# Token-major openings in 512-column halves for four feed-forward blocks and a state-space block on one Trainium2 core

## The chip, the cores and the metric

The kernel runs on one core of a Trainium2 chip. The time is the device time of one execution in microseconds (us), lower is better. Three executions of the kernel before took 1203.37, 1204.36 and 1206.2 us, a median of 1204.36 us. The profile is one further execution.

## What is computed

A decoder trunk of four layers on x of 256 tokens by 1024 features, all in float32. Each layer is a token mixer and then a feed-forward block, both behind an RMSNorm and added to x. The mixers are stick-breaking attention (layers 0 and 3), a chunked spatial gate (layer 1) and a diagonal state-space layer, S5 (layer 2). What the change touches is this part:

```python
def causal_depthwise_conv(h, w, b):
    L = h.shape[1]
    hp = jnp.pad(h, ((0, 0), (CONV_K - 1, 0), (0, 0)))
    y = hp[:, 0:L] * w[0]
    for kk in range(1, CONV_K):
        y = y + hp[:, kk:kk + L] * w[kk]
    return y + b

def conv_gated_ffn(xn, w_up, conv_w, conv_b, w_down):
    h = causal_depthwise_conv(xn @ w_up, conv_w, conv_b)
    a, g = jnp.split(h, 2, axis=-1)
    return (jax.nn.silu(g) * a) @ w_down

def s5_layer(xn, w_in, ...):
    u = (xn @ w_in).astype(jnp.float32)
    ...
    _, _, xr, xi = lax.associative_scan(_complex_affine_combine, (a_re, a_im, bu_re, bu_im), axis=1)
    ...
    hg = jax.nn.gelu(y).astype(xn.dtype) @ w_glu
    a, g = jnp.split(hg, 2, axis=-1)
    return a * jax.nn.sigmoid(g)
```

`w_up` is 1024 x 5632, `w_down` 2816 x 1024, the S5 `w_in` 1024 x 1024.

## The kernel before

**Precision.** Every large product is made of three float32r matmuls: weights and activations are each split into a high part (`wh`, `xth`, `gh`) and the rest (`wl`, `xtl`, `gl`), and high x high, high x low and low x high are added up in PSUM. ScalarE (ACT) makes `wh` from the loaded weights `raw` (L71), VectorE (DVE) makes `wl` (L72), for half of a weight chunk (128 x 1024) at a time.

**Weights.** The class `Weights` streams chunks of 128 x 2048 floats (1 MB), in the order in which the phases use them, through three `raw` buffers and six `wh`/`wl` pairs. `take()` names the next chunk; `prep_to`, `half_to` and `step` put the splitting of later chunks into the program, and with it the DMA of the chunk after. Nothing is scheduled by a planner: each engine runs its instructions in the order in which the Python code issues them, and semaphores connect the engines.

**Phases.** `K.run` goes through eight phases (attention, feed-forward, gate, feed-forward, S5, feed-forward, attention, feed-forward). Each has an opening (`head`, once per block of 128 tokens, b = 0 and b = 1), a `body`, and a `tail` that interleaves its last products with the norm of the next phase. In the opening of block 0, `mid()` puts the transposes of block 1's normed input into the middle. A matmul's output goes to one of eight PSUM banks of 128 x 512 floats.

**Feed-forward.** The 5632 columns of `w_up` are 22 chunks "u" of 256 columns: chunk m holds 128 columns of the half `a` (s = 0) and 128 of the half `g` (s = 1). From chunk 4 on a chunk is projected feature-major (`proj_feat`: the weights are the stationary operand, 256 tokens the moving one; 24 matmuls of 256 columns for each s) into one of the banks 4 to 7, in rotation. The order is u4 u5 d0 u6 u7 d1 ..., where "d" is a chunk of `w_down` (`down`, 24 matmuls of 512 columns), accumulated in banks 0 to 3. The first three chunks are projected token-major instead (`proj_tok`: 128 tokens stationary, 256 weight columns moving, 24 matmuls of 256 columns for each block), so that block 0 can begin before block 1 is normed. Their results are copied from PSUM to two tiles `tk` (L362, L363) and turned to feature-major by PE transposes (L368, four per chunk) into banks 4, 5 and 6, in the middle of the fourth chunk's `proj_feat`.

`evac` takes chunks out of PSUM: per chunk two ACT instructions with the bias (L406), four on DVE for the convolution (L410), then silu, product and the split into `gh`/`gl` (L416, L417, L198, L199). Weight halves (L71 on ACT, L72 on DVE) are issued between those steps. The bank of a chunk is free after its last L410. `evac` of a chunk is issued one step after its projection.

**S5.** The opening is that of the feed-forward for three chunks of `w_in`. In `body` the fourth chunk goes to bank 7 feature-major, with the transposes of the first three into banks 4, 5 and 6 in its middle. 48 copies (`ucopy`, L1222 on DVE and L1224 on ACT) then regroup the state-space rows from PSUM into two tiles `U` of 128 x 1024: 16 on ACT and 16 on DVE for the first, 16 on ACT for the second. `gmm(i)` (L1140) multiplies quarter i of them with tables, into banks 0 and 1 for even i and 2 and 3 for odd i. `scan(i)` is a chain of DVE instructions (L1156 to L1167), with one tile `mg` that ACT writes (L1147); `kmm`, `kd`, `kevac` build a kernel matrix, `ymm` and `yevac` the output, and `glu` the gated projection.

Of the kernel before, what the change touches and what calls it, by code (L numbers as in the profile page):

```python
# [326 lines left out]
class FFN(Phase):  # L327
# [10 lines left out]
    def open(self):  # L338
# [8 lines left out]
        self.hb = [(7, 4), (2, 3)]  # L347

    def head(self, b, mid):
        k = self.k  # L350
# [7 lines left out]
        if b == 0:  # L358
            self.tk = []
        tk = k.xn_p.tile([128, D], F32, tag="xn", name="tk")  # L360
        self.tk.append(tk)
        self.nc.scalar.activation(tk[:, 0:512], k.bank(self.hb[b][0]), AF.Copy)  # L362
        self.nc.scalar.activation(tk[:, 512:768], k.bank(self.hb[b][1])[:, 0:256], AF.Copy)  # L363

    def transposes(self, m, p):
        for b in range(2):
            for s in range(2):
                self.nc.tensor.transpose(p[:, 256 * s + 128 * b:256 * s + 128 * b + 128],  # L368
                                         self.tk[b][:, 256 * m + 128 * s:256 * m + 128 * s + 128],
                                         self.k.ident[:, :])  # L370
# [1009 lines left out]
```

## Time and profile before

| | |
|---|---|
| median of three executions | 1204.36 us |
| the profiled execution | 1203.6 us |
| its span, first to last instruction | 1201.8 us |
| PE busy | 1179.5 us |
| DVE busy | 892.8 us |
| ACT busy | 709.3 us |

The span leaves out 1.8 us of the profiled execution. PE is TensorE's matmuls, PEld its weight loads, which run beside the matmuls. [...] In rows of the timeline the columns are start, duration (from the first start to the last end where a row stands for several), engine, line, operation, output <- inputs, shapes and count; a bracket at the end tells how long the engine had been idle and what ended it. The four feed-forward phases begin at about 133, 395, 696 and 1005 us, S5 at 585 us.

### The profile page before, as it was taken

To read this page: it belongs to the slowest core of one execution; us is meant where nothing else is said; L and a number is where in the kernel's file an instruction comes from. 1 tells how busy PE (TensorE), PEld (TensorE's weight loads), DVE (VectorE), ACT (ScalarE), POOL (GpSimd) and SP (SyncE) were. 2 spreads that over 40 slices of the span, in tenths; PEclk is the share of its full clock that TensorE was granted. 3 is DMA by queue.
4 is the path that set the end of the run, shared out by engine and by line. 5 is a ranking of instruction groups with operands and counts; after the bars stand their busy time and mean duration, and the time that the engine had idled before them with its cause. 6 is when DMAs were issued, how large, how long until landed. Compare 5 with 4: busy or idle time off the path is not lost. (4 is left out here: it accounts for less than half of the span.)

```text
span 1201.8 us, 21989 instructions
## 1 busy us (share of the span) xinstructions
PE 1179.5 (98%) x9072; PEld 1078.9 (90%) x9072; DVE 892.8 (74%) x1272; ACT 709.3 (59%) x1080; POOL 152.8 (13%) x293
## 2 busy tenths in 40 slices
PE   8999999999999999999987999999999999999997
PEld 5898999999898999999976899999988989999996
DVE  5665689799767599899669759777765656886673
ACT  5665576557564564667466657556545655665551
POOL 2886000000186001000100000000000000000000
PEclk9999999999999999999999999999999999999999
DMA  8633367786655466777862646644535333565530
GB/s 297 225 106 123 132 217 282 238 308 252 245 209 182 152 222 219 227 267 259 318 250 73 261 160 218 225 179 172 199 142 204 106 124 122 203 240 180 206 124 35
DMA packets 49557, 237.46 MB, mean 198 GB/s; under 512 B 14896, under 2 KB 15792, under 8 KB 24240
## 3 DMA queue, kind: packets, MB, share of 16 engines
q1 hardware_dynamic: 46208, 223.73, 51.9%
q0 software_dynamic: 3104, 12.06, 2.5%
q8 instruction: 71, 1.16, 0.4%
q14 instruction: 30, 0.25, 0.1%
q10 hardware_dynamic: 144, 0.26, 0.1%
HBM read 222.79 MB, written 13.24 MB: 196 GB/s over the span
## 5 line engine op out<-in xcount | busy, mean ns | idle before, releaser
L72 DVE TENSOR_TENSOR wl<-raw,wh 128x1024 fp32r<-128x1024 f32 x344 | 413.6, 1227 | 56.7 <-ACT wh L71 56.6
L124 PE MATMUL pst<-xth,wh 128*128 128x256 f32 x1552 | 441.0, 284 | 0.0
L125 PE MATMUL pst<-xtl,wh 128*128 128x256 f32 x1552 | 439.1, 283 | 0.0
L126 PE MATMUL pst<-xth,wl 128*128 128x256 f32 x1552 | 439.1, 283 | 0.0
L71 ACT ACTIVATE wh<-raw 128x1024 fp32r<-128x1024 f32 x344 | 350.2, 1048 | 9.5 <-DMA raw<-in_up_dram 3.9
L124 PEld LDWEIGHTS pst<-xth,wh 128*128 128x128 f32 x1552 | 297.7, 192 | 2.3
L125 PEld LDWEIGHTS pst<-xtl,wh 128*128 128x128 f32 x1552 | 297.8, 192 | 1.2
L126 PEld LDWEIGHTS pst<-xth,wl 128*128 128x128 f32 x1552 | 297.7, 192 | 0.0
L410 DVE SCALAR_TENSOR_TENSOR y<-pst,cw,y 128x255 f32<-128x255 f32 x352 | 160.7, 479 | 72.8 <-ACT y L406 66.6
L132 PE MATMUL pst<-wh,gh 128*128 128x512 f32 x512 | 201.3, 393 | 0.0
L133 PE MATMUL pst<-wl,gh 128*128 128x512 f32 x512 | 199.8, 390 | 0.0
L134 PE MATMUL pst<-wh,gl 128*128 128x512 f32 x512 | 199.3, 389 | 0.0
L406 ACT ACTIVATE y<-pst,cw 128x256 f32<-128x256 f32 x176 | 88.0, 556 | 69.5 <-PE pst L126 64.9
L134 PEld LDWEIGHTS pst<-wh,gl 128*128 128x128 f32 x512 | 96.1, 188 | 20.4
L132 PEld LDWEIGHTS pst<-wh,gh 128*128 128x128 f32 x512 | 96.3, 188 | 19.5 <-issue 0.3
L133 PEld LDWEIGHTS pst<-wl,gh 128*128 128x128 f32 x512 | 96.3, 188 | 18.4 <-DVE wl L72 0.2
L132 PE MATMUL pst<-wh,xth 128*128 128x256 f32 (+1 forms) x336 | 105.9, 315 | 0.0
L134 PE MATMUL pst<-wh,xtl 128*128 128x256 f32 (+1 forms) x336 | 105.4, 314 | 0.0
L133 PE MATMUL pst<-wl,xth 128*128 128x256 f32 (+1 forms) x336 | 105.3, 313 | 0.0
L163 POOL TENSOR_TENSOR r<-m,mhalf 128x1 f32<-128x1 f32 x20 | 11.0, 552 | 730.5 <-DVE m L161 730.5
L198 ACT ACTIVATE gh<-y 128x256 fp32r<-128x256 f32 x88 | 36.1, 418 | 75.5 <-DVE y L417 75.5
L416 ACT ACTIVATE y<-y 128x256 f32<-128x256 f32 x88 | 36.4, 419 | 73.6 <-DVE y L410 73.4
(167 smaller groups left out, 1202.7 us busy)
## 6 DMA issues: line engine op xcount, KB each, us to landing
raw<-in_up_dram SPq DMA_DIRECT2D x88, 1024.0 KB, 4.9
raw<-in_down_dram SPq DMA_DIRECT2D x44, 1024.0 KB, 4.9
raw<-in_wqk_dram SPq DMA_DIRECT2D x16, 1024.0 KB, 4.9
raw<-in_wo_dram SPq DMA_DIRECT2D x8, 1024.0 KB, 4.7
raw<-in_glu_dram SPq DMA_DIRECT2D x8, 1024.0 KB, 6.1
raw<-in_wv_dram SPq DMA_DIRECT2D x7, 1024.0 KB, 4.9
gb<-in_g_dram SPq DMA_DIRECT2D x9, 512.0 KB, 5.6
d_gt<-gf POOLq DMA_DIRECT2D x4, 1024.0 KB, 7.8
```

What stands on the lines that cost most here:

```text
L71: nc.scalar.activation(h[:, s], r[:, s], AF.Copy)
L72: nc.vector.tensor_tensor(out=l[:, s], in0=r[:, s], in1=h[:, s], op=ALU.subtract)
L124: nc.tensor.matmul(out, h[:, cols], xh, start=first, stop=False, skip_group_check=True)
L125: nc.tensor.matmul(out, h[:, cols], xl, start=False, stop=False, skip_group_check=True)
L126: nc.tensor.matmul(out, l[:, cols], xh, start=False, stop=last, skip_group_check=True)
L132: nc.tensor.matmul(out, ah, h[:, cols], start=first, stop=False, skip_group_check=True)
L133: nc.tensor.matmul(out, ah, l[:, cols], start=False, stop=False, skip_group_check=True)
L134: nc.tensor.matmul(out, al, h[:, cols], start=False, stop=last, skip_group_check=True)
L198: self.nc.scalar.activation(g[0][:, j], src, AF.Copy)
L406: nc.scalar.activation(y[:, cs], p[:, cs], AF.Identity, scale=cw[:, s, m, 2:3], bias=cw[:, s, m, 3:4])
L410: nc.vector.scalar_tensor_tensor(y[:, o + tap:o + 256], p[:, o:o + 256 - tap], cw[:, s, m, 2 - tap:3 - tap], y[:, o + tap:o + 256], ALU.mu ...
L416: nc.scalar.activation(y[:, 256:512], y[:, 256:512], AF.Silu)
```

## The change

The first four chunks of each `w_up`, and all of the S5 `w_in`, are packed in another way: instead of 256 columns by all eight k-tiles, a 1 MB chunk now holds 512 columns by four k-tiles. All four are projected token-major with `proj_half` (which the attention and the gate used before): 12 matmuls of 512 moving columns for each chunk and block, two chunks for 512 features. The names of the lines below are those of the changed kernel; L419, L423, L429 and L430 in it are L406, L410, L416 and L417 of the kernel before, L360 is the copy L362, L372 is the transpose L368, and L366 is a new copy in the new `rest`.

```diff
     def head(self, b, mid):
...
         for c in range(3):
-            p = k.bank(self.hb[b][c // 2])
-            k.proj_tok(self.hn[c], b, p[:, 256 * (c % 2):256 * (c % 2) + 256])
+            k.proj_half(self.hn[c], c % 2, b, k.bank(self.vb[b][c // 2]))
             if c == 1:
                 mid()
...
-        self.nc.scalar.activation(tk[:, 0:512], k.bank(self.hb[b][0]), AF.Copy)
-        self.nc.scalar.activation(tk[:, 512:768], k.bank(self.hb[b][1])[:, 0:256], AF.Copy)
+                self.tk.append(k.xn_p.tile([128, D], F32, tag="xn", name="tk"))
+                self.nc.scalar.activation(self.tk[b][:, 0:512], k.bank(self.vb[b][0]), AF.Copy)
+
+    def rest(self, n, b, out):
+
+        p = self.k.bank(self.vb[b][1])
+        self.k.proj_half(n, 1, b, p)
+        self.nc.scalar.activation(out, p, AF.Copy)
...
     def body(self):
...
+        def part(m, bank):
+            self.transposes([t[:, 256 * m:256 * m + 256] for t in self.tk], k.bank(bank))
+            pend.append((m, k.bank(bank)))
+
         for kind, a in self.order()[3:-3]:
             n = w.take()
-            if kind == "u":
-                p = k.bank(4 + a % 4)
+            if kind == "u" and a == 3:
+                self.rest(n, 0, self.tk[0][:, 512:1024])
+                part(0, 5)
+                part(1, 6)
+                self.rest(n, 1, self.tk[1][:, 512:1024])
+                e = []
+            elif kind == "u":
+                p = k.bank(7 if a == 4 else 4 + (a - 3) % 4)
                 k.proj_feat(n, p, 0)
-                if a == 3:
-                    for m in range(3):
-                        self.transposes(m, k.bank(4 + m))
-                        pend.append((m, k.bank(4 + m)))
+                if a == 4:
+                    part(2, 4)
+                    part(3, 5)
                 k.proj_feat(n, p, 1)
                 e = [(a, p)]
...
 class S5(Phase):
-    tb = (0, 1)
+    tb = (2, 3)
...
     def body(self):
-        ut = k.pst[:, 4:8, :].rearrange("p b (a t) -> p (b a) t", a=2)
+        mg = self.tmp.tile([128, 8, 64], F32, name="mg")
+        xs = [[self.tmp.tile([128, 8, 64], F32, name=f"x{i}{r}") for r in range(2)] for i in range(2)]
+        ut = [k.pst[:, b:b + 2, :].rearrange("p b (a t) -> p (b a) t", a=2) for b in (0, 5)]
+        tb = [t[:, :, :].rearrange("p a c -> p (a c)") for t in xs[1]]
...
         n = w.take()
-        k.proj_feat(n, k.bank(7), 0)
-        for m in range(3):
-            FFN.transposes(self, m, k.bank(4 + m))
-        k.proj_feat(n, k.bank(7), 1)
+        FFN.rest(self, n, 0, tb[0])
+        for m in range(2):
+            FFN.transposes(self, [t[:, 256 * m:256 * m + 256] for t in self.tk], k.bank(m))
+        new_u()
+        ucopy(0, slice(0, 2), on_act)
+        ucopy(0, slice(2, 4), nc.vector.tensor_copy)
+        FFN.rest(self, n, 1, tb[1])
...
-        gb = lambda i, r: k.bank(2 * (i % 2) + r)
+        gb = lambda i, r: k.bank(2 - 2 * (i % 2) + r)
...
-        ucopy(0, slice(0, 2), on_act)
-        ucopy(0, slice(2, 4), nc.vector.tensor_copy)
         gmm(0)
+        for m in range(2):
+            FFN.transposes(self, [t[:, 256 * m:256 * m + 256] for t in tb], k.bank(5 + m))
...
         ucopy(1, slice(0, 4), on_act)
         kmm(0)
         gmm(1)
         scan(0, lambda: (kd(0), kevac(0)))
...
-        acc = [(k.bank(0), k.bank(1)), (k.bank(4), k.bank(7))]
+        acc = [(k.bank(2), k.bank(3)), (k.bank(4), k.bank(7))]
...
-        self.acc = [(k.bank(2), k.bank(3)), (k.bank(5), k.bank(6))]
+        self.acc = [(k.bank(0), k.bank(1)), (k.bank(5), k.bank(6))]
```

The first place is ACT's queue where the first feed-forward body begins, before the change. Square brackets name the semaphores that the instruction waits for; `tk_1682` is the token-major tile of block 1, `y_1753`, `y_1760` and `y_1767` are chunks 0, 1 and 2.

```order
L362 ACTIVATE tk_1682<-pst_81 128x512 [waits DVE_49,PE_49]
L363 ACTIVATE tk_1682<-pst_81 128x256 [waits PE_49]
L71 ACTIVATE wh21_1685<-raw21_1600 128x1024 [waits DMAHW1_49]
L71 ACTIVATE wh21_1685<-raw21_1600 128x1024
L406 ACTIVATE y_1753<-pst_81,cw_1505 128x256 [waits PE_49,DMAHW0_49,Activation_49,Pool_49]
L406 ACTIVATE y_1753<-pst_81,cw_1505 128x256
L406 ACTIVATE y_1760<-pst_81,cw_1505 128x256 [waits PE_49]
```

The same place with the change (`tk_1543` and `tk_1597` are blocks 0 and 1, `y_1653` and `y_1660` chunks 0 and 1):

```order
L360 ACTIVATE tk_1597<-pst_81 128x512 [waits DVE_49,PE_49]
L71 ACTIVATE wh21_1611<-raw21_1563 128x1024 [waits DMAHW1_49]
L71 ACTIVATE wh21_1611<-raw21_1563 128x1024
L366 ACTIVATE tk_1543<-pst_81 128x512 [waits PE_49]
L366 ACTIVATE tk_1597<-pst_81 128x512 [waits PE_49]
L419 ACTIVATE y_1653<-pst_81,cw_1505 128x256 [waits DMAHW0_49,Activation_49,Pool_49]
L419 ACTIVATE y_1653<-pst_81,cw_1505 128x256
```

The first chunks' evacuation (L406, now L419) now stands behind two copies L366, each of which waits for the PE to end a `rest`; before, it stood behind L363 and two weight halves.

The second place is PE's queue in the same phase, where `d0` ends (L133, L134) and u6 begins (L124), before the change:

```order
L133 MATMUL pst_81<-wl22_1775,gh_1788 128x512
L134 MATMUL pst_81<-wh22_1774,gl_1789 128x512
L124 MATMUL pst_81<-xth_1462,wh23_1798 128x256 [waits Activation_49]
L125 MATMUL pst_81<-xtl_1463,wh23_1798 128x256
L126 MATMUL pst_81<-xth_1462,wl23_1799 128x256 [waits DVE_49]
```

And with the change:

```order
L133 MATMUL pst_81<-wl22_1668,gh_1679 128x512
L134 MATMUL pst_81<-wh22_1667,gl_1680 128x512
L124 MATMUL pst_81<-xth_1462,wh23_1685 128x256 [waits DVE_49,Activation_49]
L125 MATMUL pst_81<-xtl_1463,wh23_1685 128x256
L126 MATMUL pst_81<-xth_1462,wl23_1686 128x256
```

u6 was written to bank 6, which chunk 2 had left, and is now written to bank 7, which chunk 4 leaves. Its first matmul now waits for DVE too; the count that it waits for is reached by the last convolution instruction (L423) of chunk 4.

The third place is ACT's queue in the S5 body, before the change (`U_6544` and `U_6545` are the two tiles `U`):

```order
L363 ACTIVATE tk_6463<-pst_81 128x256 [waits PE_49]
L1224 ACTIVATE U_6544<-pst_81 32x2x64 [waits PE_49,Activation_49]
L1224 ACTIVATE U_6544<-pst_81 32x2x64 x15
L1224 ACTIVATE U_6545<-pst_81 32x4x64 [waits PE_49,Activation_49]
L1224 ACTIVATE U_6545<-pst_81 32x4x64 x15
L1147 ACTIVATE mg_6546<-spar_91 128x8x63 [waits DMASW4_49,DMASW3_49,DMASW5_49,DMASW2_49,DMASW1_49]
```

With the change (`x10_6222` and `x11_6223` hold the last 512 features of blocks 0 and 1):

```order
L366 ACTIVATE x10_6222<-pst_81 128x512 [waits DMASW3_49,DMASW2_49,DMASW4_49,DMASW1_49,DMASW5_49,PE_49,Activation_49]
L1137 ACTIVATE U_6245<-pst_81 32x2x64 [waits DVE_49,PE_49,Activation_49]
L1137 ACTIVATE U_6245<-pst_81 32x2x64 x15
L366 ACTIVATE x11_6223<-pst_81 128x512 [waits PE_49]
L1137 ACTIVATE U_6343<-pst_81 32x4x64 [waits PE_49,Activation_49]
L1137 ACTIVATE U_6343<-pst_81 32x4x64 x15
L1179 ACTIVATE mg_6219<-spar_91 128x8x63
```

A copy of block 1's result out of bank 3 now stands between the two groups of 16 row copies. The second group waits for PE's last transposes of that result, which stand behind `gmm(0)` in PE's queue; `gmm(0)` writes banks 2 and 3, and its third matmul, the first into bank 3, waits for that copy.

More of the change, by code (lines that the diff above doesn't have):

```diff
@@ L352, in head, with transposes @@
             self.hn = [k.w.take() for _ in range(3)]
+            self.tk = []
         for c in range(3):
-            p = k.bank(self.hb[b][c // 2])
-            k.proj_tok(self.hn[c], b, p[:, 256 * (c % 2):256 * (c % 2) + 256])
+            k.proj_half(self.hn[c], c % 2, b, k.bank(self.vb[b][c // 2]))
             if c == 1:
                 mid()
[L358 to L362, printed above, removed]
-        self.nc.scalar.activation(tk[:, 512:768], k.bank(self.hb[b][1])[:, 0:256], AF.Copy)
-    def transposes(self, m, p):
+                self.tk.append(k.xn_p.tile([128, D], F32, tag="xn", name="tk"))
[4 more added lines that the diff above has]
+        self.nc.scalar.activation(out, p, AF.Copy)
+    def transposes(self, tk, p):
         for b in range(2):
@@ L1148, in scan @@
             x = X[i]
-            b = k.pst[:, 2 * (i % 2):2 * (i % 2) + 2].rearrange("p r (a c) -> p r a c", a=8)
+            b = k.pst[:, 2 - 2 * (i % 2):4 - 2 * (i % 2)].rearrange("p r (a c) -> p r a c", a=8)
             t = [self.tmp.tile([128, 2, 8, 64], F32, tag=f"t{n}", name=f"t{n}") for n in range(2)]
@@ L1213, in yevac @@
             nc.vector.tensor_tensor(out=g[1][:, :, :], in0=y[:, :, :], in1=g[0][:, :, :], op=sub)
-        def ucopy(h, cols, copy):
-            d = U[h].rearrange("p (m r) c -> p m r c", m=4)
-            for pr in range(4):
-                for j in range(4):
-                    m = slice(4 * h + cols.start, 4 * h + cols.stop)
-                    src = ut[32 * pr:32 * pr + 32, m].rearrange("p m (c j) -> p m c j", j=4)[:, :, :, j]
-                    copy(d[32 * j:32 * j + 32, cols, pr, :], src)
-        on_act = lambda o, i: nc.scalar.activation(o, i, AF.Copy)
-        for h in range(2):
-            U.append(k.xn_p.tile([128, D], F32, tag="xn", name="U")[:, :].rearrange("p (a c) -> p a c", a=16))
         K_, X_ = (None,), (0, 1)
-        mg = self.tmp.tile([128, 8, 64], F32, name="mg")
-        xs = [[self.tmp.tile([128, 8, 64], F32, name=f"x{i}{r}") for r in range(2)] for i in range(2)]
         X = {i: xs[i % 2] for i in range(4)}
+        gmm(0)
+        for m in range(2):
+            FFN.transposes(self, [t[:, 256 * m:256 * m + 256] for t in tb], k.bank(5 + m))
         for t in [mg] + xs[0] + xs[1]:
             nc.gpsimd.memset(t[:, :, 0:1], 0.0)
-        ucopy(0, slice(0, 2), on_act)
-        ucopy(0, slice(2, 4), nc.vector.tensor_copy)
-        gmm(0)
+        new_u()
         ucopy(1, slice(0, 4), on_act)
```

24 lines of the change are left out of this document (17 added, 7 removed).

## The prediction

> **What bounds the kernel now.** I read the page first: engine shares and the slices of the span.
>
> ```profile
> span 1201.8 us, 21989 instructions
> PE 1179.5 (98%) x9072; PEld 1078.9 (90%) x9072; DVE 892.8 (74%) x1272; ACT 709.3 (59%) x1080; POOL 152.8 (13%) x293
> PE   8999999999999999999987999999999999999997
> ```
>
> PE has work nearly everywhere; the two weaker slices in the middle are S5. Busy time by stretch says what kind of bound each place has (length, then the engines' busy time, clock and DMA share):
>
> ```profile
> 586.00:611.00 25.00, 25.00 (x213) 24.87 (x213) 9.02 (x19) 9.84 (x22) 5.56 (x9) 1.00 1.00 407
> 611.00:664.00 53.00, 43.06 (x1207) 35.16 (x1208) 49.07 (x57) 35.94 (x73) 0.00 (x0) 1.00 0.29 110
> 692.00:860.00 168.00, 167.99 (x1238) 160.14 (x1237) 125.80 (x194) 100.97 (x156) 0.55 (x1) 1.00 0.52 188
> ```
>
> A feed-forward phase (692 to 860) is PE from end to end: whatever makes PE's stream shorter or puts a wait into it counts in full. In S5 (611 to 664) DVE is busy 49 of 53 us, PE 43: there only what starts DVE's scans earlier or later counts. The list of waits agrees: no PE wait is on a convolution (L410), so today every bank is free in time.
>
> **PE's stream in a feed-forward phase.** Starts of matmuls in the third such phase: its first, two ends of a dense 256-column stretch with the twelve transposes behind it, and the first of `d0` and of u6.
>
> ```profile
> 696.45 0.28 PE L132 MATMUL pst<-wh,xth 128*128 128x256 f32 x1
> 702.20 1.04 PE L179 MATMUL pst<-ident,xn 128*128 128x128 f32 x8
> 703.00 0.36 PE L132 MATMUL pst<-wh,xth 128*128 128x256 f32 x1
> 703.20 0.28 PE L133 MATMUL pst<-wl,xth 128*128 128x256 f32 x1
> 717.46 1.47 PE L368 MATMUL pst<-ident,tk 128*128 128x128 f32 x12
> 718.69 0.36 PE L124 MATMUL pst<-xth,wh 128*128 128x256 f32 x1
> 733.17 0.40 PE L132 MATMUL pst<-wh,gh 128*128 128x512 f32 x1
> 738.64 0.28 PE L124 MATMUL pst<-xth,wh 128*128 128x256 f32 x1
> ```
>
> From 703.20 to 717.46 run 119 matmuls of 256 columns, 0.120 us each; `d0` is 24 of 512 columns from 733.17 to 738.64, 0.228 us each. So the wide form is worth 2 x 0.120 - 0.228 = 0.012 us per pair, though its instruction count halves. The first four chunks are 192 narrow matmuls now (23.0 us) and 96 wide ones then (21.9 us): 1.1 us saved. Eight transposes cost 0.88 us (0.80, and 0.08 because the first matmul behind them takes 0.20), twelve 1.31. After the change 16 stand there in two groups: 1.76, so 0.45 us is given back. **Net gain of PE's own work: 0.7 us per phase**, 3 us in four.
>
> [...]
>
> **What the gain runs into.** The next rows are DVE and ACT at the same place: the PE matmul behind the one that ACT's copy in the opening waits for, that copy, the fourth and fifth chunks' weight halves, the evacuation of chunks 0, 1 and 2, the convolutions of the same chunks and of chunk 4, the one extra DVE instruction in the first feed-forward phase, and the busy time of PE, PEld, DVE, ACT and POOL from 719.3 to 738.
>
> ```profile
> 711.70 0.28 PE L132 MATMUL pst<-wh,xth 128*128 128x256 f32 x1
> 711.90 0.60 ACT L362 ACTIVATE tk<-pst 128x512 f32<-128x512 f32 x1 [1.59 <-PE pst L134]
> 707.50 4.63 DVE L72 TENSOR_TENSOR wl<-raw,wh 128x1024 fp32r<-128x1024 f32 x4 [2.75 <-ACT wh L71]
> 718.24 2.84 ACT L406 ACTIVATE y<-pst,cw 128x256 f32<-128x256 f32 x6 [1.18 <-PE pst L368]
> 719.29 5.54 DVE L410 SCALAR_TENSOR_TENSOR y<-pst,cw,y 128x255 f32<-128x255 f32 x12 [0.78 <-ACT y L406]
> 735.02 1.00 ACT L406 ACTIVATE y<-pst,cw 128x256 f32<-128x256 f32 x2
> 736.06 1.91 DVE L410 SCALAR_TENSOR_TENSOR y<-pst,cw,y 128x255 f32<-128x255 f32 x4
> 168.35 0.43 DVE L956 STREAM_TRANSPOSE wt<-spar 128x256 f32<-128x256 f32 x1
> 719.30:738.00 18.70, 18.70 (x139) 17.86 (x139) 18.34 (x35) 14.04 (x25) 0.00 (x0) 1.00 0.54 184
> ```
>
> DVE starts the convolutions at 719.29 and ends chunk 4's at 736.06 + 1.91 = 737.97: 18.68 us almost without a gap (the last row: DVE busy 18.34 of 18.70) for five chunks' convolutions (20 L410) and, between them, six weight halves and four chunks' gating. The change batches this as chunks 0-1, 2-3, 4 instead of 0-1-2, 3, 4, with the same instructions and the same six halves, so I keep 18.7 us; adding up my own order of the steps I get 18.9.
>
> Now the starts, counted from 696.45. PE: 24 wide matmuls 5.47, eight transposes 0.88, 60 wide matmuls 13.68, eight transposes 0.88, 12 wide matmuls 2.74. The last `rest` ends at 720.10; before, the same work ended 96 narrow matmuls (11.5) ahead of 733.17, at 721.67. Only then may ACT copy that result, and the copy is ahead of L406 (now L419) in its queue: start 0.2 later (711.90 against 711.70), 0.6 for the copy, less 0.1 overlap, 1.0 for two L406: 721.8. DVE starts at about 721.85, **2.55 us later than before**, and ends chunk 4 at 740.5.
>
> PE meanwhile needs: first half of u4 2.88, transposes 0.44, a wait of some 0.35 for bank 5 (chunk 0's convolution ends 721.85 + 1.91 = 723.76), transposes 0.44, second half 2.88, u5 5.75, `d0` 5.47: it stands at u6 at 738.3. u6's bank is 7, chunk 4's, in use until 740.5. Before, u6 took chunk 2's bank, long free. With 0.07 for the semaphore u6 starts at 740.6 instead of 738.64: **PE waits 2.3 us and the phase is 2.0 us longer**. The head start of 1.6 us at 720.10 is lost in this wait, since the DVE chain hangs on the end of `rest`. Behind u6, u7 and u8 take the banks of chunks 2 and 3, free by then, and from u9 on the rotation is the old one. In the first phase L956 lies in the stretch (0.37 with its gap): 2.3 there. Sum: 3 x 2.0 + 2.3 = **8.3 us**. Bounds: no wait at all gives -0.7 per phase (-2.8), 18.9 instead of 18.7 and 0.005 us more or less per wide matmul give 1.5 to 2.7 per phase (6.3 to 11.1). I take 8.3, built from the nearest rows.
>
> **S5.** PE's first matmul and transposes, the row copies (ACT's two groups, DVE's one), where PE waited for them, a whole `gmm` (615.73 to 617.64, 1.9 us), and the start of the scans:
>
> ```profile
> 585.62 0.28 PE L132 MATMUL pst<-wh,xth 128*128 128x256 f32 x1
> 606.63 1.47 PE L368 MATMUL pst<-ident,tk 128*128 128x128 f32 x12
> 607.98 4.89 ACT L1224 ACTIVATE U<-pst 32x128 f32<-32x128 f32 x17 [3.65 <-PE pst L368]
> 607.99 4.84 DVE L1222 COPY U<-pst 32x128 f32<-32x128 f32 x16 [14.06 <-PE pst L368]
> 612.53 0.34 PE L1140 MATMUL pst<-U,wh 128*64 128x64 f32 x4 [0.69 <-ACT U L1224]
> 612.50 6.21 ACT L1224 ACTIVATE U<-pst 32x256 f32<-32x256 f32 x16
> 615.73 0.34 PE L1140 MATMUL pst<-U,wh 128*64 128x64 f32 x4
> 617.64 0.23 PE L1140 MATMUL pst<-U,wh 128*64 128x64 f32 x2
> 618.74 0.62 ACT L1147 ACTIVATE mg<-spar 128x504 f32<-128x504 f32 x1
> 619.45 2.34 DVE L1162 TENSOR_TENSOR_SCAN t<-mg,t 128x512 f32<-128x512 f32 x2 [1.59 <-issue]
> 660.24 1.10 PE L1201 MATMUL pst<-x,wh 128*32 128x64 f32 x64 [2.61 <-DVE x L1166]
> ```
>
> DVE waited 1.59 us before its first scan (L1162) for `mg`, the instruction behind ACT's 32 row copies; from there its rows follow one another up to 660, where PE waits for them. So S5 is set by **when ACT ends the row copies**. After the change: transposes at 585.62 + 5.47 + 0.88 + 13.68 = 605.65. ACT may overwrite `tk` after the sixth of them (before, after the tenth: 0.1 us apart, copies 0.43 behind it), at 606.6; 16 copies take 612.50 - 607.98 = 4.52, to 611.1. Next in ACT's queue is the copy of `rest(1)`, 0.6, to 611.7. `gmm(0)` had the PE at 605.65 + 0.88 + 2.74 = 609.3, but its third matmul writes the bank that this copy empties: PE waits 2.4 us, then takes 1.9, to 613.6. Only then come the transposes for the second tile (eighth issued 0.72 later, 0.43 to ACT), so ACT starts the other 16 copies at 614.8, ends at 621.0 (6.21), `mg` at 621.6, and the first scan starts at about 621.7 instead of 619.45: **2.2 us later**, which the DVE chain hands on in full. The copies beside the last projection run there, but ACT then idles from 611.7 to 614.8 with the other half not yet transposed. Bounds: with no wait at all on ACT (the 1.59 us gone and the first copies done 1.4 earlier) -3.0; with 0.3 more at each of the five hand-overs +3.7.
>
> Hidden: the longer ACT copies, since ACT idles there; and the fourth chunk's weights, whose halves end by 712.1 (707.50 + 4.63) today and are wanted by `rest` at 713.7 instead of 714.6. The S5 tables are the other thing that PE could find missing:
>
> ```profile
> 618.00:620.00 2.00, 1.25 (x35) 1.03 (x32) 0.55 (x1) 1.92 (x5) 0.00 (x0) 1.00 0.84 321
> 620.00:622.00 2.00, 1.58 (x51) 1.51 (x54) 1.97 (x3) 1.93 (x4) 0.00 (x0) 1.00 0.17 61
> ```
>
> The DMA engines are full until about 620 (share 0.84, then 0.17): the last tables land then. The same number of bytes is asked for, a little sooner, and the second scan, which reads the last of them, comes later; so I cost this at nothing, and at up to 1 us, which PE would wait for the second half's tables, if the order of landing changes.
>
> **Sum.** 8.3 + 2.2 = 10.5 us on the profiled execution's 1203.6 us (span 1201.8 and 1.8 around it): 1214.1. That execution lies 0.8 us under the median of 1204.36; for the median I say **1214.5**.
>
> **The rivals.**
> (1) *No new wait decides.* DVE has 26% of the span free; if its backlog at u6 were shorter by 2.3 us, and ACT's second group no later, PE's shorter stream and the earlier scans would show: 1204.4 - 2.8 - 3.0 = 1198.6, faster. It decides the other way once chunk 4's convolution ends before 738.3. Against it: the DVE rows leave only 0.36 us free between 719.3 and 738 and begin 2.55 us later.
> (2) *Only the banks are free*, S5 as computed: 1204.4 - 2.8 + 2.2 = 1203.8, no change.
> (3) *Only S5 gains*, the feed-forward waits as computed: 1204.4 + 8.3 - 3.0 = 1209.7.
> (4) *The clock falls in the new waits*, of 2.3 us four times and 2.4 once. The trace has a case of either kind (two stretches at the kernel's start, and the PE row ahead of them):
>
> ```profile
> 9.33 1.48 PE L179 MATMUL pst<-ident,xn 128*128 128x128 f32 x8 [2.84 <-DVE xn L155]
> 10.00:12.00 2.00, 2.00 (x8) 1.09 (x9) 0.21 (x1) 2.00 (x5) 0.44 (x1) 0.59 1.02 428
> 12.00:14.00 2.00, 2.00 (x7) 0.80 (x6) 1.85 (x3) 1.67 (x3) 0.12 (x1) 0.56 1.04 434
> ```
>
> Behind a wait of 2.84 us, with a PE that had little to do before, the granted clock is 0.59 and 0.56 for 4 us; behind the 2.61 us before 660.24 it is 1.00. If each of the five waits cost what the first did, 4 x 0.43 = 1.7 us, the time would be 1214.5 + 8.6 = 1223. The new waits are shorter than both and lie in a dense stream, so I give it little. [...]
>
> **How the numbers follow.** The likeliest case, both waits, 0.70, in 1211 to 1218. Rival (3) 0.11, (1) 0.06, (2) 0.07, (4) 0.06. Leaving out (1), (2) and (4), with 0.19, the range is 1209 to 1218. A measurement of this kernel can tell about 0.2% (2.4 us) from no change. Faster by more: (1), 0.06. Within: (2), 0.07. Slower by more: the rest, 0.87.
>
> **What would show it.** In each feed-forward phase of the changed profile: a PE wait of about 2 us at u6's first matmul (L124) released by DVE's L423, one of 0.3 to 0.5 before the transposes of chunk 3, and 512-column matmuls 0.228 us apart in the opening. In S5: a PE wait of about 2.4 us inside `gmm(0)` on ACT's L366, ACT idle some 3 us between its groups of row copies, and the first scan some 36 us after S5's first matmul (33.8 before). Wrong would be: no PE wait at u6; an opening that is several us shorter; first scan under 34 us after the start; or a clock below 1.00 behind the waits.

## The result, and the profile after

| | before | changed |
|---|---|---|
| median of six executions | 1203.84 us (1202.72 to 1206.20) | 1217.62 us (1216.69 to 1219.89) |
| ratio | | 1.0114 (95%: 1.0103 to 1.0126) |

The change makes the kernel 13.8 us slower; 10.5 were forecast on the profiled execution, 10.1 on the median. The sign and the range were right, the size was 3.1 us short (1217.62 against 1214.5).

The sixth execution of the changed kernel, the one that was profiled, ran at a mean clock of 0.749 and took 1443.05 us; it counts in the median (1217.56 without it), but not in the range and the ratio. The rows below are therefore of another execution of the same kernel, 1216.78 us long, with a span of 1215.0, the fastest of four (e1_again, below). Its page, engine shares and slices:

```profile
span 1215.0 us, 21073 instructions
PE 1182.9 (97%) x8612; PEld 1061.4 (87%) x8612; DVE 892.6 (73%) x1272; ACT 711.7 (59%) x1080; POOL 150.7 (12%) x293
...
PE   8999999999999999999988999999999999999997
...
PEclk9999999999999999999998999999999999999999
```

PE has 460 matmuls fewer and is busy 3.4 us *longer*; DVE and ACT have nearly the same work as before. The page averages too much to say more, except for one digit: PEclk has an 8 in the slice in which S5 lies, where the page of before had only nines. The list of PE's waits (us in total, times, longest) is where the change shows first:

```profile
PE pst L124 <- DVE y L423: 8.5, 4, 2.4
...
PE pst L1172 <- ACT x L366: 2.0, 1, 2.0
...
PE pst L372 <- DVE y L423: 1.3, 4, 0.3
```

None of the three is in the list of before. They are the waits at u6, inside `gmm(0)`, and before the transposes of chunk 3. The third feed-forward phase again, in rows of the timeline (it starts at 704.16 here; L419 and L423 are bias and convolution; wide matmuls overlap in these rows, 0.39 us long and 0.23 us from start to start, so what one costs is read from the starts):

```profile
704.16 0.39 PE L132 MATMUL pst<-wh,xth 128*128 128x512 f32 x1
704.39 0.39 PE L133 MATMUL pst<-wl,xth 128*128 128x512 f32 x1
704.62 0.39 PE L134 MATMUL pst<-wh,xtl 128*128 128x512 f32 x1
...
724.10 1.03 PE L372 MATMUL pst<-ident,tk 128*128 128x128 f32 x8
727.92 0.60 ACT L366 ACTIVATE tk<-pst 128x512 f32<-128x512 f32 x1 [3.02 <-PE pst L134]
728.42 1.93 ACT L419 ACTIVATE y<-pst,cw 128x256 f32<-128x256 f32 x4
729.47 3.73 DVE L423 SCALAR_TENSOR_TENSOR y<-pst,cw,y 128x255 f32<-128x255 f32 x8 [6.67 <-ACT y L419]
731.52 0.63 PE L372 MATMUL pst<-ident,tk 128*128 128x128 f32 x4 [0.33 <-DVE y L423]
746.24 1.90 DVE L423 SCALAR_TENSOR_TENSOR y<-pst,cw,y 128x255 f32<-128x255 f32 x4
748.29 0.36 PE L124 MATMUL pst<-xth,wh 128*128 128x256 f32 x1 [2.04 <-DVE y L423]
```

Read it from the bottom: u6 starts when chunk 4's convolution ends (746.24 + 1.90 = 748.14, and 0.15 from there to u6); that chain began at 729.47, behind ACT's bias instructions, which stood behind the copy at 727.92, which waited for PE's last `rest`. The transposes of chunks 0 and 1 had been there since 724.10 + 1.03. DVE was idle for 6.67 us ahead of its first convolution.

S5, which starts at 590.61 here: its first matmul, ACT's copies, PE's wait in `gmm(0)`, `mg` and the first scan:

```profile
590.61 0.39 PE L132 MATMUL pst<-wh,xth 128*128 128x512 f32 x1
611.46 4.49 ACT L1137 ACTIVATE U<-pst 32x128 f32<-32x128 f32 x16
615.97 0.60 ACT L366 ACTIVATE x<-pst 128x512 f32<-128x512 f32 x1
616.62 0.34 PE L1172 MATMUL pst<-U,wl 128*64 128x64 f32 x4 [2.02 <-ACT x L366]
619.71 6.22 ACT L1137 ACTIVATE U<-pst 32x256 f32<-32x256 f32 x16 [3.14 <-PE pst L372]
625.95 0.62 ACT L1179 ACTIVATE mg<-spar 128x504 f32<-128x504 f32 x1
626.66 2.34 DVE L1194 TENSOR_TENSOR_SCAN t<-mg,t 128x512 f32<-128x512 f32 x2 [4.07 <-issue]
```

The first scan starts 36.05 us after S5's first matmul; before it was 33.83. All of this is as computed. What the prediction did not have is in the busy times by stretch (length, busy PE, PEld, DVE, ACT, POOL, clock, DMA) around the u6 of the third and of the fourth phase:

```profile
744.00:746.00 2.00, 2.00 (x10) 1.51 (x9) 2.00 (x5) 1.79 (x5) 0.00 (x0) 1.00 0.00 0
746.00:748.00 2.00, 0.25 (x2) 0.00 (x0) 1.93 (x5) 1.50 (x3) 0.00 (x0) 1.00 0.33 123
748.00:750.00 2.00, 1.71 (x10) 1.74 (x11) 2.00 (x4) 1.05 (x3) 0.00 (x0) 0.70 0.95 401
750.00:752.00 2.00, 2.00 (x11) 2.00 (x11) 1.96 (x5) 1.92 (x4) 0.00 (x0) 0.50 0.26 33
1058.00:1060.00 2.00, 0.74 (x4) 0.27 (x2) 1.97 (x6) 1.50 (x3) 0.00 (x0) 1.00 0.37 66
1060.00:1062.00 2.00, 1.23 (x10) 1.26 (x11) 1.96 (x4) 1.17 (x2) 0.00 (x0) 1.00 0.96 401
1062.00:1064.00 2.00, 2.00 (x19) 2.00 (x18) 1.97 (x4) 1.88 (x4) 0.00 (x0) 1.00 0.17 66
```

Behind the wait of the third phase the granted clock is 0.70 and 0.50, and PE gets through 11 matmuls in 2 us where it gets through 19 at full clock. Behind the same wait in the fourth phase it stays at 1.00. PE counts as busy either way, 2.00 of 2.00 us at 0.50 (from 750) as at 1.00 (from 1062): a slower clock cannot be seen in the shares of busy time.

### The profile page after: what moved, and what is told of

Its sections match the earlier page's. It is cut to its first block, busy times and chain, and to the rows that moved or that the text cites. A ratio compares the mean times of both kernels' runs of the same rounds, so it can differ in the third digit from the quotient of the medians.

```text
span 1441.3 us, 21073 instructions
## 1 busy us (share of the span) xinstructions
PE 1422.8 (99%) x8612; PEld 1197.6 (83%) x8612; DVE 896.9 (62%) x1272; ACT 717.1 (50%) x1080; POOL 141.4 (10%) x293
## 4 chain that ended last, share of the span: by engine, by line
PE 97%; ACT 2%; DMA 0%; issue 0%; DVE 0%; SPq 0%; DVEq 0%; POOLq 0%; ACTq 0%
PE pst L132 15%; PE pst L133 15%; PE pst L134 15%; PE pst L125 15%; PE pst L126 15%; PE pst L124 14%; PE pst L179 1%; PE pst L549 1%; PE pst L525 1%; PE pst L1233 1%; PE pst L372 1%; PE pst L566 1%; ACT U L1137 1%; DMA gb<-in_g_dram 0%; ACT kk L1220 0%; ACT wl L1220 0%
## 5 line engine op out<-in xcount | busy, mean ns | idle before, releaser
L126 PE MATMUL pst<-xth,wl 128*128 128x256 f32 x1472 | 464.7, 316 | 0.0
L124 PE MATMUL pst<-xth,wh 128*128 128x256 f32 x1472 | 463.2, 315 | 0.0
L124 PEld LDWEIGHTS pst<-xth,wh 128*128 128x128 f32 x1472 | 323.2, 220 | 4.0
L126 PEld LDWEIGHTS pst<-xth,wl 128*128 128x128 f32 x1472 | 324.4, 220 | 0.0
L423 DVE SCALAR_TENSOR_TENSOR y<-pst,cw,y 128x255 f32<-128x255 f32 x352 | 160.8, 479 | 201.8 <-ACT y L419 195.3
L132 PE MATMUL pst<-wh,gh 128*128 128x512 f32 x512 | 237.4, 464 | 0.0
L134 PE MATMUL pst<-wh,gl 128*128 128x512 f32 x512 | 233.8, 457 | 0.0
L133 PE MATMUL pst<-wl,gh 128*128 128x512 f32 x512 | 233.7, 456 | 0.0
L419 ACT ACTIVATE y<-pst,cw 128x256 f32<-128x256 f32 x176 | 88.6, 560 | 184.6 <-PE pst L126 184.6
L134 PEld LDWEIGHTS pst<-wh,gl 128*128 128x128 f32 x512 | 102.5, 200 | 43.3
L133 PEld LDWEIGHTS pst<-wl,gh 128*128 128x128 f32 x512 | 103.7, 203 | 38.6
L133 PE MATMUL pst<-wl,xth 128*128 128x512 f32 x256 | 118.6, 463 | 0.0
L132 PE MATMUL pst<-wh,xth 128*128 128x512 f32 x256 | 117.2, 458 | 0.0
L134 PE MATMUL pst<-wh,xtl 128*128 128x512 f32 x256 | 116.2, 454 | 0.0
L134 PEld LDWEIGHTS pst<-wh,xtl 128*128 128x128 f32 x256 | 51.6, 201 | 21.7 <-DVE xtl L186 0.4
```

Of the source, the lines that this page charges most:

```text
L124: nc.tensor.matmul(out, h[:, cols], xh, start=first, stop=False, skip_group_check=True)
L126: nc.tensor.matmul(out, l[:, cols], xh, start=False, stop=last, skip_group_check=True)
L132: nc.tensor.matmul(out, ah, h[:, cols], start=first, stop=False, skip_group_check=True)
L133: nc.tensor.matmul(out, ah, l[:, cols], start=False, stop=False, skip_group_check=True)
L134: nc.tensor.matmul(out, al, h[:, cols], start=False, stop=last, skip_group_check=True)
L419: nc.scalar.activation(y[:, cs], p[:, cs], AF.Identity, scale=cw[:, s, m, 2:3], bias=cw[:, s, m, 3:4])
```

## The experiments

Times are medians, with range and number of executions; the ratio is against the kernel before, run on the same chip beside them (its median was 1204.3 to 1204.7 each time).

| kernel | time, us | ratio (95%) |
|---|---|---|
| e1_again, the change | 1220.51 (1216.78 to 1221.35, 4) | 1.0129 (1.0104 to 1.0155) |
| e2_rotation | 1208.44 (1206.45 to 1211.04, 10) | 1.0030 (1.0018 to 1.0042) |
| e3_ffn_alone | 1217.19 (1214.19 to 1220.03, 4) | 1.0099 (1.0070 to 1.0129) |
| e4_s5_alone | 1209.31 (1207.49 to 1211.15, 10) | 1.0039 (1.0027 to 1.0050) |
| e5_filler | 1214.97 (1214.40 to 1216.10, 4) | 1.0087 (1.0073 to 1.0101) |
| e6_early | 1204.20 (1201.88 to 1205.14, 10) | 0.9996 (0.9987 to 1.0005) |
| e7_mg_first | 1220.50 (1216.54 to 1221.90, 4) | 1.0123 (1.0101 to 1.0144) |
| e8_early_mg | 1206.38 (1203.30 to 1209.14, 11) | 1.0013 (1.0003 to 1.0023) |
| e9_early_s5_before | 1202.44 (1201.02 to 1206.56, 12) | 0.9987 (0.9977 to 0.9997) |
| e10_kmm_first | 1205.82 (1203.63 to 1206.96, 12) | 1.0011 (1.0002 to 1.0020) |
| e11_s5_filled | 1208.08 (1203.13 to 1209.46, 8) | 1.0031 (1.0019 to 1.0042) |
| e12_short_filler | 1215.39 (1213.08 to 1216.13, 5) | 1.0085 (1.0071 to 1.0098) |

From each profile come the lengths of the phases, each from its first matmul to that of the next phase (the last to the start of the span's last instruction), and the stretches at half clock that the trace lists, without those in the first and the last 20 us of the span. A stretch lasts 3.4 us, where "x2" stands 6.8.

| kernel | feed-forward 1 to 4, us | S5, us | half clock from, us |
|---|---|---|---|
| before | 189.78, 189.78, 189.78, 196.30 | 110.83 | none |
| e1_again | 192.12, 193.28, 193.27, 198.29 | 113.55 | 441.6, 632.7, 646.4 x2, 748.8 |
| e2 | 190.83, 190.65, 189.52, 196.03 | 115.51 | 614.1, 631.2, 648.2 |
| e3 | 192.12, 193.27, 191.79, 198.31 | 112.43 | 444.0, 641.9, 665.8 |
| e4 | as before | 117.61 | 611.1, 628.2, 638.4, 662.3 x2 |
| e5 | 192.10, 191.82, 191.77, 198.29 | 114.51 | 616.3, 633.3 |
| e6 | 188.99, 188.99, 188.99, 195.50 | 115.39 | 611.2, 628.2, 641.9 x2 |
| e7 | 192.11, 193.27, 193.25, 198.29 | 116.75 | 443.2, 634.3, 648.0 x2, 665.0, 753.8 |
| e8 | as e6 | 115.89 | 639.9 x2, 657.0 |
| e9 | as e6 | 113.27 | 658.0 x2 |
| e10 | as e6 | 117.06 | 618.7 x2, 639.2 x2, 656.2 |
| e11 | as e6 | 113.96 | 626.7 |
| e12 | 192.11, 191.83, 191.80, 198.30 | 114.06 | 631.5, 648.6 |

### The change once more, and its halves

e1_again is the changed kernel. e3 and e4 each take one half of the change, e3 the feed-forward phases, e4 S5, with the packing of the weights that belongs to it:

```diff
# e3: class S5 and a["ssin"] as before the change, with its own old opening
+class Old:
+    def head(self, b, mid):
...
# e4: class FFN and a["up"] as before the change; S5 with the new opening
+class New:
+    def head(self, b, mid):
...
```

e2 changes one line of the changed kernel, the bank of the chunks from u4 on:

```diff
-                p = k.bank(7 if a == 4 else 4 + (a - 3) % 4)
+                p = k.bank((7, 6, 4, 5)[(a - 4) % 4])
```

With it u6 takes bank 4, which chunk 2 leaves, not bank 7.

> The changed kernel once more, for a profile at full clock. It took 13.8 us more than the kernel before, where the prediction's sum was 10.5. Theory A (the two waits, each only longer than computed, clock 1.00 behind them): PE waits of 2 to 3 us at u6 in each feed-forward phase and about 2.4 us in gmm(0), PEclk 1.00 in the 6 us behind them, and the missing 3 us lie in longer waits. Theory B (rival 4 in part: the waits are as computed, and the granted clock falls behind some of them): waits of 2.0 to 2.4 us, granted clock under 0.9 for some 3 to 4 us behind at least two of the five, about 1.7 us lost behind each. About 1217.5 us in both.

> The changed kernel with another bank order from u4 on (7, 6, 4, 5, 7, ...): u6 takes the bank of chunk 2 instead of that of chunk 4. Nothing else differs. If the wait at u6 is what makes the feed-forward phases longer, each of them becomes 0.4 to 0.7 us shorter than in the kernel before and only S5's +2.2 is left: 1203 to 1205 us (theory A), the same plus up to 1.7 where the clock falls in S5 (theory B): 1204 to 1207. If the wide matmuls themselves or the copies cost the time: 1212 or more.

> The feed-forward part of the change alone, S5 as before. By the prediction +8.3: 1212. Theory A with longer waits in the feed-forward phases: up to 1215. Theory B: 1212 plus 1.7 for each phase in which the clock falls, 1214 to 1218.

> The S5 part of the change alone, feed-forward as before. By the prediction +2.2: 1206.0. Theory B with a clock fall behind gmm(0): up to 1207.7. If the 3 us that the prediction lacked lie in S5: 1209.

The feed-forward half makes 12.5 us (1217.19 less 1204.65), S5 4.7: each is more than its term of 8.3 and 2.2, and together, 17.2, they are a little more than the whole beside them (15.9, 1220.51 less 1204.65; this median of the changed kernel is 2.9 us over its first one). The rotation alone takes away 12.1 of the whole (1220.51 less 1208.44). In its profile DVE still starts late, but nothing waits for it at u6:

```profile
745.32 0.39 PE L134 MATMUL pst<-wh,gl 128*128 128x512 f32 x1
745.55 0.28 PE L124 MATMUL pst<-xth,wh 128*128 128x256 f32 x1
```

The first matmul of u6 (745.55) follows the last of d0 after 0.23 us, 41.93 us into the phase. So the feed-forward loss hangs on the wait at u6, and that is a matter of which bank. But 12 us is more than the 8.3 that four such waits sum to. The table of phases tells where the rest is: against before, e1_again's phases are longer by 2.34, 3.50, 3.49 and 1.99 us, of which u6's delay (at 44.45, 44.12, 44.12 and 44.12 us after the phase's start, 42.19 before) is 2.26 and three times 1.93. The two phases with 1.5 us more are those with a half-clock stretch directly behind u6, from 441.6 and 748.8. In e3 it is one phase, the second. e2's own remainder, 0.9 to 1.1 us in the first two phases, is two later waits for `gh` and `gl`; by it, and by an S5 that is 4.7 us longer than before, e2 misses its forecast of at most 1207.

S5 has the same at its new wait, the one in `gmm(0)`. In e1_again and e12 the first scan starts 36.05 and 36.03 us after S5's start; in e2, e4, e5 and e6, whose S5 is the same code, it starts at 37.55, 37.55, 37.47 and 37.57. In these four a stretch at half clock begins within 1.1 us of the end of that wait (at 614.1, 611.1, 616.3 and 611.2); in e1_again and e12 none begins before 41 us into S5. Two stretches and the first scan of e6, whose S5 starts at 584.11:

```profile
608.00:610.00 2.00, 0.10 (x4) 0.00 (x0) 1.92 (x7) 1.92 (x7) 0.00 (x0) 1.00 1.03 426
612.00:614.00 2.00, 2.00 (x21) 1.88 (x19) 1.15 (x2) 0.00 (x0) 0.00 (x0) 0.50 0.98 407
...
621.68 2.34 DVE L1197 TENSOR_TENSOR_SCAN t<-mg,t 128x512 f32<-128x512 f32 x2 [4.73 <-ACT mg L1182]
```

What is then left of `gmm(0)` and the transposes behind it run at half clock, so ACT's second group of row copies starts 30.6 us after S5's start instead of 29.1, and the scan is 1.5 us later with it.

### Is it the clock? PE filled during the wait

e5 leaves the wait as it is and gives PE matmuls to do in it, into a free bank; their results are not used. e12 does the same with 3 instead of 8.

```diff
                 k.down(self.gt[a], n, self.acc, (0, 1), a == 0, False)
+                if a == 0:
+                    for _ in range(8):
+                        k.nc.tensor.matmul(k.bank(4), self.gt[0][0][:, 1, 128:256], w.hl[n][0][:, 1536:2048],
+                                           start=True, stop=True, skip_group_check=True)
```

> The changed kernel with eight more matmuls of 512 columns (results not used) between d0 and u6 of each feed-forward phase, into bank 4, which chunk 2 has left. The wait for bank 7 stays, but PE works through 8 x 0.228 = 1.8 of its 2.0 to 2.4 us. Theory (the wait is as computed, and what was missing in the sum is the clock, which fell to half behind two of the four waits in the profile of the changed kernel and cost 1.5 us each time): u6 starts as before at 44.1 us after the phase's start (44.4 in the first), no clock fall stands behind it in any phase, the four phases take 192.1, 191.8, 191.8 and 198.3 us, and the time is 1.5 to 3 us below the changed kernel's 1217.6: 1214.6 to 1216.1. Rival (the missing us are in the wait or in what follows it, not in the clock): phases of 193.3 us again in the second and third, 1217.6 or, if the extra matmuls delay u6, more.

> The changed kernel with three instead of eight unused matmuls between d0 and u6: 0.7 us of the wait are filled, 1.35 us stay empty (1.7 in the first phase). In the profiles so far the clock fell to half behind a window of 3.41 us in a dense stretch when PE was without a matmul for 2.04 us of it (three cases), and not when it was for 1.75, 1.61, 1.36 or 1.26. Theory (a threshold between 1.75 and 2.04 us of one window): no fall behind u6 in any phase, u6 at 44.1 us after the phase's start, 1214.4 to 1216.1 as with eight. Rival (what the eight matmuls took away is not a fall but the emptiness itself, or the threshold is lower): a fall in some phases, 1216.5 to 1219.

Two rows that are the same place in two kernels, u6 of the third phase, first of e5:

```profile
749.09 0.36 PE L124 MATMUL pst<-xth,wh 128*128 128x256 f32 x1 [0.22 <-DVE y L427]
```

and of e12:

```profile
748.36 0.36 PE L124 MATMUL pst<-xth,wh 128*128 128x256 f32 x1 [1.35 <-DVE y L427]
```

L427 in these kernels is the convolution L423. u6 starts at 44.11 and 44.12 us after the phase's start, as in the changed kernel, so nothing was gained in waiting. Yet both kernels are faster than it by 2.6 and 2.2 us (1217.62 less 1214.97 and 1215.39), with twelve and more unused products in the four phases. No stretch at half clock is left in any feed-forward phase, and those phases are 8.3 and 8.4 us longer than before in sum (e5: 773.98 less 765.64), against 11.3 in e1_again. The slowest execution of either (1216.13) is below the fastest of the changed kernel in both of its runs (1216.69). The clock in e5, at the place where it was 0.70 and 0.50:

```profile
748.00:750.00 2.00, 1.78 (x12) 1.32 (x11) 1.96 (x5) 1.37 (x2) 0.00 (x0) 1.00 0.94 385
750.00:752.00 2.00, 2.00 (x19) 2.00 (x18) 2.00 (x5) 1.56 (x4) 0.00 (x0) 1.00 0.33 131
```

That what the feed-forward phases lacked in the sum, some 3 us, is the clock is therefore shown. The times also spread with it: the four executions of e3, with the mean clock of each, are 1214.19 us (0.996), 1215.55 (0.992), 1218.83 (0.988) and 1220.03 (0.988); those of e5 lie within 1.7 us. e12 shows that the wait need not be filled: 1.35 us of emptiness (1.68 in the first phase, 1.41 in the second) do nothing, 2.04 us do behind two of the three such waits in e1_again.

### Is it DVE's late start? The evacuation ahead of the copy

e6 has the change's own banks, with u6 on chunk 4's. Only ACT's order is different: its copy of the second `rest` is issued behind the bias instructions of chunks 0 and 1.

```diff
-                self.rest(n, 1, self.tk[1][:, 512:1024])
+                k.proj_half(n, 1, 1, k.bank(self.vb[1][1]))
+                mid = lambda: k.nc.scalar.activation(self.tk[1][:, 512:1024], k.bank(self.vb[1][1]), AF.Copy)
...
-            self.evac(pend)
-            pend = e
+            self.evac(pend, mid)
+            pend, mid = e, nop
```

`evac` calls `mid()` behind the convolutions' loop.

> The changed kernel, only that in the feed-forward body ACT's copy of the second rest stands behind the bias instructions of chunks 0 and 1 instead of ahead of them. u6 still takes chunk 4's bank. Theory (DVE's convolutions start late because ACT waits for the second rest first, and the wait at u6 is DVE's backlog): the convolutions start at some 22 us after the phase's start instead of 25.3, the backlog of 18.7 us ends at some 40.7, ahead of PE's 41.6, and the wait at u6 and the one before chunk 3's transposes go; phases of 189.1 to 189.6 us, 1204.5 to 1209 in all with S5 as changed. Rival (it is the bank's rotation alone, and DVE's backlog grows back in the same stretch): u6 waits 2 us again, 1215 to 1219.

The same place in e6 (third phase from 699.50; L421 is the bias, L425 the convolution, L391 the moved copy):

```profile
720.21 1.93 ACT L421 ACTIVATE y<-pst,cw 128x256 f32<-128x256 f32 x4
721.27 3.73 DVE L425 SCALAR_TENSOR_TENSOR y<-pst,cw,y 128x255 f32<-128x255 f32 x8 [3.14 <-ACT y L421]
723.26 0.60 ACT L391 ACTIVATE tk<-pst 128x512 f32<-128x512 f32 x1 [1.11 <-PE pst L134]
738.04 1.90 DVE L425 SCALAR_TENSOR_TENSOR y<-pst,cw,y 128x255 f32<-128x255 f32 x4
740.67 0.39 PE L134 MATMUL pst<-wh,gl 128*128 128x512 f32 x1
740.90 0.28 PE L124 MATMUL pst<-xth,wh 128*128 128x256 f32 x1
```

DVE starts 21.77 us after the phase's start instead of 25.31, works the same 18.67 us (721.27 to 739.94), and is done 0.96 us ahead of u6. Both new waits are gone, the phases are 0.79 us *shorter* than before, and the whole is level with before, S5's loss included: the late start is the cause, and the bank only decides who pays for it. The rival fell.

### A version that beats both

e9 is e6 with S5 as before the change.

> The feed-forward openings as changed with the early evacuation of chunks 0 and 1, S5 as before the change. Theory (with the wait gone a feed-forward phase is 0.79 us shorter than before, S5 before takes 110.8 us, or 112.4 where the clock falls in it): four times 0.79 off the kernel before, 1201.2, or up to 1202.8 with falls in S5: the first kernel here that is faster than before. Rival (S5 as before behind the new openings always has falls, or the opening of another phase loses): 1203.5 to 1205.

1202.44 us, within the forecast and 1.9 us under the kernel before, with an interval that ends just under no change. Every feed-forward phase has its 0.79 us; the profile's S5 has 6.8 us at half clock and takes 113.27. Against e6, S5 as changed costs 1.8 us. In the profiles S5 varies by more than that between executions of one and the same code (110.83 before, 112.43 in e3, 113.27 in e9).

### S5: three edits that gained nothing

e7 issues `mg` of the first scan ahead of ACT's second group of row copies; e8 is e7 and e6 together; e10 is e8 with `kmm(0)` ahead of `gmm(0)`; e11 is e8 with unused matmuls where PE waits in S5.

```diff
# e7, e8, e10, e11
+        set_mg(0)
         ucopy(1, slice(0, 4), on_act)
# e10
+        kmm(0)
         gmm(0)
...
-        kmm(0)
         gmm(1)
# e11: two ahead of gmm(0), one ahead of gmm(2), one in ymm(0) and one in ymm(1), two ahead of the last part of ymm(3)
+        fill(5, tb[0], 2)
         gmm(0)
...
+                nc.tensor.matmul(k.bank(b), k.ident[:, :], src, start=True, stop=True, skip_group_check=True)
```

> The changed kernel, only that in S5 the mg of the first scan is written by ACT ahead of the second group of row copies instead of behind it. Theory (the first scan waits only for mg, 4.07 us, behind ACT's second group of row copies): the first scan starts 32.0 us after S5's first matmul (36.05 in the changed kernel's profile, 33.83 before), S5 takes some 109.5 us instead of 113.5 where the clock falls nowhere in it, and the time is 2 to 4 us below the changed kernel's: 1213.5 to 1215.6. Rival (the row copies decide by the products that read them, or the tables by their landing): the first scan is early, but the second or third waits, and the time stays at 1216.5 to 1218.5.

> Both edits together: the evacuation of chunks 0 and 1 ahead of the copy of the second rest, and mg ahead of the second group of row copies. Theory: the two gains add up, 9 to 13 us in the feed-forward phases and 2 to 4 in S5 below the changed kernel: 1201 to 1206.5, so level with or faster than the kernel before (1204.4). Rival: one of them is eaten by the next wait, 1207 to 1210.

> Early evacuation and mg ahead of the second row copies, and in S5 the kernel matrix products (kmm(0), 1.95 us) ahead of gmm(0) instead of behind it, so that PE works while ACT frees bank 3. Theory (in S5 the waits cost more than they last, by the clock that falls to half behind those that fill over 1.9 us of a window of 3.4; the window of this wait goes): the wait of 2.0 us in gmm(0) goes, no clock fall there, S5 1 to 3 us shorter than with mg first alone (115.9), 1203.5 to 1205.5 in all. Rival (the tables for kmm have not landed yet at 23.7 us after S5's start, or PE's later waits set the end alone): no gain, 1206 or more.

> Early evacuation and mg ahead of the second row copies, and in S5 matmuls whose results are not used, 0.9 us each, where PE waits: two ahead of gmm(0), one each ahead of gmm(2) and of the last parts of the first two output products, two ahead of the last part of the fourth. Theory (the clock, not the waits, eats what the earlier first scan gains): fewer falls in S5, S5 at 108 to 111 us instead of 115.9, 1199 to 1202.5. Rival (PE is short of time in S5 by itself, by its many small products and their instructions): 1205 or more, S5 at 114 or more in spite of a full clock.

In e8, whose S5 starts at 584.91, the first scan, the gap in PE's products (a stretch at half clock follows it from 657.0), and the last DVE instruction of the output products:

```profile
616.79 2.33 DVE L1202 TENSOR_TENSOR_SCAN t<-mg,t 128x512 f32<-128x512 f32 x2
...
656.36 0.65 PE L1241 MATMUL pst<-U,wl 128*32 128x64 f32 x30 [2.97 <-issue]
...
668.05 0.69 DVE L1253 TENSOR_TENSOR gl<-y,gh 128x512 fp32r<-128x512 f32 x1 [5.75 <-ACT gh L1252]
```

The first scan starts 31.88 us after S5's start, 4.2 us earlier than in e1_again, as expected. But the last `gl` is 83.14 us after it, where before it was 78.49 (664.11 less 585.62) and in e1_again 80.71: DVE now waits 5.75 us for ACT, which waits for PE's last products. So with the scans early it is PE that ends S5, and e7 (the time of e1_again, and above both of its forecasts) and e8 (2.2 us over e6) gain nothing; that e8 lies within its forecast is owed to e6's edit alone. e10's wait in `gmm(0)` is gone, as it should be, the clock stays up behind it and falls 8 us later, and S5 is no shorter (117.06). In e11's profile the clock is whole but for one stretch and S5 still takes 113.96, with the unused matmuls themselves in it (the two ahead of `gmm(0)` leave 0.3 us of a wait that is 2.0 in e8, so some 0.9 each); the other seven executions are 3.7 to 6.3 us longer than that one. So of the theory "the clock eats it" only part can be held: PE loses by the clock, by a gap of 2.97 us for which the profile has no releaser, and by its own work behind the second tile, and I cannot say in which shares.

## Why the prediction was right, and where it fell short

- **PE's own gain, 0.7 us per phase.** Right: e6, without the waits, gains 0.79. Wide matmuls start 0.23 us apart in the opening too, and d0 starts 36.46 us into the phase (36.38 computed).
- **DVE 2.55 us late, a backlog of 18.68 us.** Right: 25.31 against 22.84 us after the phase's start is 2.47 later, and from 729.47 to 748.14 are 18.67. That the batches change (0-1, 2-3, 4) costs nothing.
- **u6 at 44.15 us, a phase 2.0 us longer, 2.3 in the first.** Right: 44.12 and 44.45; the four phases without a fall of the clock are longer by 8.3 (e5), the term of 8.3.
- **0.35 us before chunk 3's transposes.** Right: 0.33.
- **S5: `gmm(0)` waits, ACT idles 3 us, the first scan 2.2 us later.** Right in the profile of e1_again: 2.02 us (2.4 computed, counted from the next slot), 3.14, and 2.22; the last `gl` is 2.22 later too, so the DVE chain hands it on in full, as was said. S5 is 2.72 longer there, and 3.23 in e12. But in these two profiles the clock stays up behind the wait in `gmm(0)`; in the other four of this S5 it falls there, the first scan is 3.6 to 3.7 later, and S5 3.7 to 6.8 longer (e5, e4). So the 2.2 is the term without a fall. By the medians S5 costs 4.7 in e4, and 1.8 between e6 and e9. That DVE's chain ends S5 holds for the change itself, but PE's chain is nearly as long, as e7 and e8 show.
- **The tables, at nothing.** Right: none of PE's waits in S5 is put down to a DMA.
- **The step that failed** is rival (4), "the new waits are shorter than both and lie in a dense stream, so I give it little". I had it as all or nothing, five falls or none, with a chance of 0.06; a clock below 1.00 behind the waits was among my signs of being wrong. It happened in part: behind two of the four waits at u6 in e1_again, at 1.5 us each (193.28 less 191.82; 1.7 computed), and in four of six profiles behind the fifth, in `gmm(0)`. The sum lacked a term of some 3 us: 2.65 between the medians of the changed kernel and of e5.
- **The step from the sum to the median.** 10.5 on the median of 1204.36 is 1214.9; the 1214.5 that I said lies between that and the 1214.1 of the profiled execution.

The row on which I relied, 2.61 us of waiting before 660.24 with the clock at 1.00 behind it, was read without the place of the wait. In all traces the stretches at half clock begin at whole multiples of 3.413 us from one another: in e1_again 441.6, 632.7, 646.4 and 748.8 are 56, 4 and 30 such steps apart, and in the kernel before the two stretches at the ends, at 10.4 and 1198.2, are 348. So each trace has a grid of steps, with an edge every 3.413 us, and these waits can be told apart by how long PE is empty within one step (where an edge cuts a wait, its longer part is given):

| wait | the part in one step, us | clock behind it |
|---|---|---|
| e1_again and e7, u6 of phases 2 and 3 | 2.04, 2.04 and 2.03, 2.04 | half |
| e3, u6 of phase 2 | 2.04 | half |
| e1_again, u6 of phases 1 and 4 | 1.75, 1.36 (an edge at 175.4, at 1059.4) | full |
| e7, u6 of phases 1 and 4 | 1.45, 1.22 | full |
| e3, u6 of phases 1, 3 and 4 | 1.61, 1.26, 1.18 | full |
| e12, u6 of phase 2 | 1.41 | full |
| e2, e4, e5, e6, `gmm(0)` | 1.99, 1.94, 1.81, 2.02 | half |
| e1_again, e7, e8, e12, `gmm(0)` | 1.08, 1.38, 1.72, 1.75 | full |
| before, ahead of 660.24 | 1.25 and 1.36 (an edge at 658.9) | full |
| e3, e9, the same wait of S5 as before, 3.49 and 4.00 long | 2.71, 2.79 | half |

The 2.61 us on which I relied were cut in two by an edge; in e3 and e9, with the same S5, the larger part of this wait lay in one step, and the clock fell. In this table the clock stays up behind parts of up to 1.75 us and falls behind parts from 1.81 us on, so for these waits the threshold T lies between the two. If T is 1.8 for every such wait, one of w makes the clock fall unless an edge cuts it into two parts under T. For that the edge has to lie in a stretch of (2T - w) out of the 3.41 us. So the chance of a fall is 0.54 for w = 2.04 and 0.64 for 2.36: 2.3 falls in four phases, or 3.4 us, and 0.8 us more in `gmm(0)`. This is an estimate made after the fact, from the traces that it explains. 8.3 + 2.2 + 4.2 is 14.7 us; 13.8 were measured, and 15.9 in e1_again.

## What to carry over

When an operation is put ahead of another in an in-order queue, follow what the second one releases: here a copy of 0.6 us, put ahead of the first evacuation, delayed another engine's backlog by 2.5 us (3.5 against e6, where it stands behind) and a third engine by 2 us, 18 us after the copy. A new wait on a PE that is otherwise full can cost more than its length, as here, where two of the four waits at u6 in e1_again, 2.04 us each, cost 1.5 us more: add the chance of a fall of the clock, or shorten the wait (a bank, an order, some useful matmul moved into it) to the 1.75 us or less behind which the clock stayed up here. When a stage has two chains of nearly the same length, making one of them 4 us shorter may bring nothing, as the first scan of e8, 4.2 us earlier than in e1_again, brought S5 none; look at both ends before counting on it.

## What was not expected of the hardware

- The grid of 3.413 us and the threshold between 1.75 and 1.81 us above, shown for the new waits by nine profiles, two of them with fillers. Among S5's matmuls of 64 columns the clock also fell behind steps in which PE's matmuls leave only 0.6 to 1.2 us empty (e11 at 626.7, e6 at 628.2, e1_again at 632.7), and stayed up behind 1.8 (e9, from 630.7); what is counted there these runs do not show.
- Extra matmuls whose results are not used made the changed kernel 2.2 (e12) and 2.6 us (e5) faster.
- The gap of 2.97 us in e8 has no releaser in the profile; a packet of 16 KB of the queue that carries instructions (q8) runs from 654.09 for 0.98 us inside it, between the two runs of small matmuls. That PE waited there for its own instructions is a guess that was not tried.
